# A unit's last product, issued behind the next unit's first two, in the gate/up loops of a two-layer trunk

## The chip, the cores and the metric

One core of a Trainium2 chip runs the whole program. The metric is device time in microseconds (us) for one execution. In the profile the engines are PE (TensorE matmul), PEld (TensorE's weight loads), DVE (VectorE), ACT (ScalarE), POOL (GpSimd) and SP, whose queue issues most of the loads.

## The reference, cut to what matters

A sequence of 512 tokens with 1024 channels passes two layers. Each layer is a token mixer and then a dense SwiGLU block; both sub-layers have an RMS norm before and after and a shift, a scale and a gate computed from a conditioning vector. The part that the change touches is the first half of the SwiGLU block, `silu(h @ w_gate) * (h @ w_up)`:

```python
D_MODEL, SEQ, D_FF = 1024, 512, 2816

def swiglu(h, w_gate, w_up, w_down):
    return (jax.nn.silu(h @ w_gate) * (h @ w_up)) @ w_down

    # in reference(), for each of the two layers i
    h = rms_norm(x, ffn_pre_g[i]) * (1.0 + scale) + shift
    y = swiglu(h, ffn_w_gate[i], ffn_w_up[i], ffn_w_down[i])
    x = x + gate * rms_norm(y, ffn_post_g[i])
```

All inputs are float32.

## The kernel before, in words

Every float32 operand is split into a high and a low part (`split`: ACT copies the high part to a `...h` tile, DVE subtracts to get the `...l` tile), and every product is three matmuls: high by high, high by low, low by high (`mm3`). Weights come from HBM in 512 KB blocks, on SP's queue, and are split on the way.

The gate and up matrices are cut into 22 blocks of 128 columns each. The first three blocks (`NH = 3`) go through `unit`, in the plain way. The other 19 go through `seven`, a Strassen-like scheme: for a pair (gate block, up block), seen as a 2 x 2 matrix of halves of the contraction by gate and up, and for the tokens in two halves of 256, seven products of half-size matrices take the place of eight. Each product is four slices of the contraction by three matmuls, so twelve matmuls of 128 x 128 weights by 256 tokens; a unit of seven products is 84 matmuls. The unit's weights are the raw halves (`x` and `b21`) and sums of them (`f13`, `f24`) that DVE makes and that are then split like the rest.

A unit uses three PSUM banks. `R1` takes A11·B11, then 2·T2 on top, then 3·T3 on top, then A22·T4 on top; `R2` takes A12·B21; `R3` takes 1·T1 and then 4·B22 on top. After most of these additions the running value is read: ACT copies `R1` and `R3` into the tile `e` (columns `s1`, `u1`, `s5`), and DVE makes four 256-column parts of `gu` from the bank and the copy. So the next product into a bank has to wait until its last reader is done. The last read before A22·T4 is DVE's `gu<-e,r`, the subtraction `s5 - R1`. A22·T4 stands in a function of its own, `rest`, which also takes the two silu's (ACT) and the product of gate and up (DVE, the tile `act`). In the kernel before, `run` calls `rest` at once after the other six products.

What sets the order: the program is written in one order, and a scheduler places each engine's instructions by their dependences, in an order fixed before the run. Where `pe["chain"]` is set, `pe_op` gives each matmul a dependence on the one written before it, so that TensorE keeps the written order; `dve.chain` and `act.chain` would do the same for their engines. None of them is set in the gate/up loops of the kernel before. Each engine then works through its own queue in order and waits on semaphores.

The loop also carries background work: after two of every three units, `bg0.step(1)` advances the computation of a modulation vector (the post-norm gate: a 512 KB load `rawada` into a slot, and a multiply-add `G<-rawada,sc,G` on DVE, eight of each in a loop, then two small splits and two pairs of 512-wide matmuls, `adaps`).

After the loop of layer 0 comes `out_proj` (the down projection, tiles `y`, weights `raw<-in_wdown`), in which two `rawada` loads are issued for each block of weights; after that of layer 1 comes `last` (tiles `X`, `M`).

In the traces all matmuls have line L90, all of DVE's and ACT's work has line L64, all DMA issues L107, and the three banks are all called `r`.

Of the kernel before, what the change touches and what calls it, by code (L numbers as in the profile page):

```python
# [25 lines left out]
def trunk(ctx: ExitStack, tc: tile.TileContext, A: dict, out: bass.AP):  # L26
# [16 lines left out]
    def nm(s):  # L43
        uid[0] += 1
        return f"{s}_{uid[0]}"

    def slot(dt, name, a=2, b=512):
        return s4.tile([P, a, b], dt, tag="s4", name=nm(name))

    def bank(name, tag="b"):  # L50
        return psum.tile([P, 512], F32, tag=tag, bufs=6 if tag == "b" else 2, name=nm(name))

    pe = {"prev": None, "chain": False}
# [47 lines left out]
    def mm3(o, lh, ll, rh, rl, start, stop):  # L101
        mm(o, lh, rh, start, False)
        mm(o, lh, rl, False, False)
        mm(o, ll, rh, False, stop)
# [101 lines left out]
    def wget(src, look=3):  # L206

        n = taken[0]
        taken[0] += 1
        while len(got) < min(n + 1 + look, len(stream)):  # L210
            wemit()
        assert stream[n][3] == src, (stream[n][3], src)
        return got[n]
# [200 lines left out]
    def hB(hT, k, lo, n):  # L414

        h, l = hT[lo // 256, k // 4]
        lo %= 256
        return h[:, k % 4, lo : lo + n], l[:, k % 4, lo : lo + n]
# [604 lines left out]
    def act_split(src):  # L1023
        t = slot(F32R, "as")
        split(t[:, 0, :], t[:, 1, :], src)
        return t[:, 0, :], t[:, 1, :]
# [5 lines left out]
    class Ffn:  # L1032
# [31 lines left out]
        def first(self):  # L1064
            return [lambda f=f: self.unit(f, 0, 256, 2 if f != 1 else 0) for f in range(NH)]

        def seven(self, f):

            W = wget(("blocks", (self.li, f - NH)), 1)
            R1, R2, R3 = [bank(n)[:, :256] for n in ("r1", "r2", "r3")]
            S = {n: (lambda k, t=self.S[n]: (t[0][:, k, :], t[1][:, k, :])) for n in "1234"}
            S["A11"] = lambda k: hB(self.hT, k, 0, 256)
            S["A12"] = lambda k: hB(self.hT, k + 4, 0, 256)
            S["A22"] = lambda k: hB(self.hT, k + 4, 256, 256)

            def product(o, a, b, start, stop):
                for k in range(4):  # L1080
                    h, l = S[a](k)
                    wh, wl = W[b](k)
                    mm3(o, wh, wl, h, l, start and k == 0, stop and k == 3)

            e = fpool.tile([P, 3, 256], F32, tag="e", name=nm("e"))
            gu = npool.tile([P, 2, T], F32, tag="n", name=nm("gu"))
            lo, hi = slice(0, 256), slice(256, T)
            s1, u1, s5 = [e[:, i, :] for i in range(3)]
            product(R1, "A11", "B11", True, False)
            act.activation(s1, R1, AF.Copy)  # L1090
            product(R2, "A12", "B21", True, True)
            dve.tensor_tensor(gu[:, 0, lo], R2, s1, ALU.add)
            product(R3, "1", "T1", True, False)
            act.activation(s5, R3, AF.Copy)
            product(R1, "2", "T2", False, False)
            act.activation(u1, R1, AF.Copy)
            product(R3, "4", "B22", False, True)
            dve.tensor_tensor(gu[:, 1, lo], R3, u1, ALU.subtract)
            product(R1, "3", "T3", False, False)
            dve.tensor_tensor(gu[:, 1, hi], s5, R1, ALU.subtract)  # L1100

            def rest():
                product(R1, "A22", "T4", False, True)
                act.activation(gu[:, 0, lo], gu[:, 0, lo], AF.Silu)
                last_act[0] = act.activation(gu[:, 0, hi], R1, AF.Silu)
                if f // 2 == len(self.act):
                    self.act.append(slot(F32, "act"))
                dve.tensor_tensor(
                    self.act[f // 2][:, f % 2, :], gu[:, 0, :], gu[:, 1, :], ALU.mult
                )  # L1110

            return rest

        def run(self, bg0, bg, bg2, steps, nhT, nxt, nS=None):
            for f in range(NH):
                self.unit(f, 256, 256)()
            for f in range(NH, KF):
                self.seven(f)()
                if f % 3:
                    bg0.step(1)  # L1120
            bg0.step(99)
            if self.li == 1:
                return self.last()
            out_proj(
                self.s, KF, lambda k: act_split(self.act[k // 2][:, k % 2, :]),
                lambda k: ("wdown", self.li, k), 4, bg, nhT, nxt, None, nS, steps, bg2,
            )


        def last(self):  # L1130
# [113 lines left out]
            for half in range(2):  # L1244
                X = [bank("X") for _ in range(NT)]
                M = [bank("M", "b" if i < 2 else "p") for i in range(4)]
                left = sum(k in "sx" for k, _ in LAST[half])
                tail = items[-NLAST:] if half else []
                while n < len(items) and items[n][0] == half and items[n] not in tail:
                    ahead(n)  # L1250
                    _, kind, j = items[n]
                    n += 1
                    if kind == "o":
                        plain(X, half, j, range(NT))
                    else:
                        seven(X, M, half, j, "mx" if kind == "s" else kind)
                        left -= kind != "m"
                        if left == 0:
                            K = joined(M)
                            left = -1  # L1260
                if half:
                    break
                junk = unread()
                for tt in range(NT):
                    dve.tensor_tensor(K[tt], X[tt][:], K[tt], ALU.add)
                    sq[0].append(small.tile([P, 1], F32, tag="sq0", name=nm("sq")))
                    act.activation(junk[:, halves[0]], K[tt], AF.Square, accum_out=sq[0][tt][:])
                    dve.tensor_tensor(K[tt], K[tt], ada["G", 3][:, halves[0]], ALU.mult)
                Y = K
# [271 lines left out]
```

## Time and profile before

| | |
|---|---|
| median of three runs | 1111.35 us |
| the profiled execution: its own time, and its span | 1111.05 us, 1109.3 us |
| PE busy | 1090.0 us, 98% of the span, 7318 matmuls |
| DVE, ACT busy | 902.3 us (81%), 603.1 us (54%) |
| gate/up loop of layer 0 | from 293.5 to 483.8 us |
| gate/up loop of layer 1 | from 797.5 to 988.2 us |
| granted TensorE clock, mean | 0.995 |

Matmuls are pipelined, so one of 256 columns is listed with 276 to 281 ns while the next one starts 113 to 118 ns after it; the pace is read from the starts of successive matmuls, not from their durations. A busy PE is for the same reason not a PE at its best pace. Idle time stands in front of the instruction that had to wait, with the name of what released it.

### The profile page before, as it was taken

How to read it: one execution, taken by the hardware profiler on the slowest of the kernel's cores; microseconds unless marked ns; L12 is line 12 of the kernel's file. 1: busy time of each engine (PE TensorE's matmuls, PEld its weight loads, DVE VectorE, ACT ScalarE, POOL GpSimd, SP SyncE). 2: the span in 40 equal slices, each digit the busy share in tenths (PEclk: the TensorE clock that was granted, in tenths of full speed). 3: DMA queues.
4: the chain of work that ended last, by engine and by line, in shares of the span. 5: the costliest groups of instructions: out<-in, count | busy, mean ns of one | idle time of the engine just before them, and what ended most of it. 6: DMA issues, size and time to landing. Idle time of an engine off the chain costs nothing.

```text
span 1109.3 us, 18286 instructions
## 1 busy us (share of the span) xinstructions
PE 1090.0 (98%) x7318; PEld 986.3 (89%) x7318; DVE 902.3 (81%) x1161; ACT 603.1 (54%) x977; POOL 39.7 (4%) x71
## 2 busy tenths in 40 slices
PE   7999999999999999999999999999999999999997
PEld 5788888789999999988878988989999999989896
DVE  7777889759998989797687774659988998889986
ACT  7746767646555555562244634437555555556552
POOL 0220111000000000010000000000000000000000
PEclk9999999999999999999999999999999999999999
DMA  9685445353344444378874582333244444223323
GB/s 362 234 240 161 147 144 163 135 190 134 97 132 153 151 138 131 96 239 266 281 254 174 181 287 87 110 130 134 79 153 129 138 134 153 76 77 109 102 95 152
DMA packets 51299, 176.09 MB, mean 159 GB/s; under 512 B 5644, under 2 KB 6156, under 8 KB 50319
## 3 DMA queue, kind: packets, MB, share of 16 engines
q1 hardware_dynamic: 45166, 153.95, 42.3%
q0 software_dynamic: 6048, 20.98, 6.0%
q8 instruction: 57, 0.93, 0.3%
q14 instruction: 28, 0.22, 0.1%
HBM read 164.43 MB, written 8.39 MB: 156 GB/s over the span
## 4 chain that ended last, share of the span: by engine, by line
PE 80%; DVE 7%; DMA 5%; issue 2%; ACT 2%; DVEq 0%; ACTq 0%
PE r L90 28%; PE y L90 11%; PE X L90 7%; PE pqk L90 7%; PE gu L90 6%; PE v L90 6%; PE u L90 4%; DMA rawada<-in_ada 3%; PE M L90 3%; PE z L90 2%; PE av L90 2%; DMA raw<-in_wdown 2%; PE tw L98 2%; DVE f L64 1%; DVE wl L64 1%
## 5 line engine op out<-in xcount | busy, mean ns | idle before, releaser
L64 ACT ACTIVATE wh<-raw 128x1024 fp32r<-128x1024 f32 (+1 forms) x112 | 117.1, 1053 | 132.4 <-DMA raw<-in_wdown 42.5
L64 DVE TENSOR_TENSOR wl<-raw,wh 128x1024 fp32r<-128x1024 f32 (+1 forms) x112 | 134.9, 1211 | 60.0 <-ACT wh L64 58.9
L90 PE MATMUL r<-Sh,wh 128*128 128x256 f32 x608 | 169.0, 278 | 0.4 <-ACT e L64 0.4
L90 PE MATMUL r<-Sh,wl 128*128 128x256 f32 x608 | 169.0, 278 | 0.0
L90 PE MATMUL r<-Sl,wh 128*128 128x256 f32 x608 | 168.9, 278 | 0.0
L90 PE MATMUL y<-wh,as 128*128 128x512 f32 x480 | 151.5, 393 | 0.0
L64 DVE TENSOR_TENSOR wl<-f,wh 128x1024 fp32r<-128x1024 f32 x76 | 92.8, 1221 | 35.5 <-ACT wh L64 35.5
L64 ACT ACTIVATE wh<-f 128x1024 fp32r<-128x1024 f32 x76 | 80.8, 1063 | 68.5 <-PE r L90 65.1
L90 PEld LDWEIGHTS r<-Sh,wl 128*128 128x128 f32 x608 | 114.8, 189 | 0.0
L90 PEld LDWEIGHTS r<-Sh,wh 128*128 128x128 f32 x608 | 114.3, 188 | 0.6 <-ACT e L64 0.6
L90 PEld LDWEIGHTS r<-Sl,wh 128*128 128x128 f32 x608 | 114.3, 188 | 0.0
L90 PEld LDWEIGHTS y<-wh,as 128*128 128x128 f32 x480 | 90.6, 189 | 18.9
L90 PE MATMUL y<-wl,as 128*128 128x512 f32 x240 | 94.2, 393 | 0.0
L90 PE MATMUL r<-hTh,wh 128*128 128x256 f32 x304 | 88.6, 291 | 1.2 <-DVE gu L64 0.6
L90 PE MATMUL r<-hTl,wh 128*128 128x256 f32 x304 | 84.4, 278 | 0.0
L90 PE MATMUL r<-hTh,wl 128*128 128x256 f32 x304 | 79.6, 278 | 0.0
L90 PE MATMUL X<-wh,as 128*128 128x512 f32 (+1 forms) x272 | 75.1, 353 | 0.0
L64 ACT ACTIVATE e<-r 128x256 f32<-128x256 f32 x114 | 43.3, 380 | 47.9 <-PE r L90 47.8
L90 PEld LDWEIGHTS r<-hTh,wh 128*128 128x128 f32 x304 | 57.2, 188 | 7.9 <-DVE gu L64 6.7
L64 ACT ACTIVATE wh<-rawx 128x1024 fp32r<-128x1024 f32 x38 | 40.4, 1063 | 35.8 <-PE r L90 30.0
L90 PE MATMUL r<-hTh,b 128*128 128x256 f32 x304 | 58.7, 278 | 0.0
L90 PEld LDWEIGHTS r<-hTl,wh 128*128 128x128 f32 x304 | 57.2, 188 | 0.1
(240 smaller groups left out, 2837.8 us busy)
## 6 DMA issues: line engine op xcount, KB each, us to landing
rawada<-in_ada SPq DMA_DIRECT2D x56, 512.0 KB, 4.6
raw<-in_wdown SPq DMA_DIRECT2D x44, 512.0 KB, 3.9
rawy<-in_wy SPq DMA_DIRECT2D x38, 512.0 KB, 3.6
rawx<-in_wx SPq DMA_DIRECT2D x38, 512.0 KB, 4.7
rawada<-in_ada POOLq DMA_DIRECT2D x24, 512.0 KB, 4.5
raw<-in_wqk SPq DMA_DIRECT2D x16, 512.0 KB, 3.9
ada<-in_ada0w SPq DMA_DIRECT2D x7, 1026.0 KB, 10.7
raw<-in_wgu SPq DMA_DIRECT2D x12, 512.0 KB, 3.6
```

Source lines behind the costliest of these rows:

```text
L64: b = f(*a, **k)
L90: b = nc.tensor.matmul(o, l, r, start=start, stop=stop, skip_group_check=True)
L98: last_tp[0] = nc.tensor.transpose(o, i, ident)
```

## The change

`seven` no longer issues its last product itself: `run` hands the `rest` of the unit before to it as `late`, and `seven` calls it behind the new unit's A11·B11 and A12·B21 and the reads that follow them. The last unit's `rest` is called after the loop. `pe["chain"]` is set for the whole loop, so that TensorE keeps the written order in it.

```diff
-        def seven(self, f):
+        def seven(self, f, late=None):
...
             act.activation(s1, R1, AF.Copy)
             product(R2, "A12", "B21", True, True)
             dve.tensor_tensor(gu[:, 0, lo], R2, s1, ALU.add)
+            if late is not None:
+                late()
             product(R3, "1", "T1", True, False)
...
             for f in range(NH):
                 self.unit(f, 256, 256)()
+            pe["chain"], late = True, None
             for f in range(NH, KF):
-                self.seven(f)()
+                late = self.seven(f, late)
                 if f % 3:
                     bg0.step(1)
+            late()
+            pe["chain"] = False
             bg0.step(99)
```

**TensorE at the first unit boundary of layer 0.** `r1_473` is the first bank of the first unit, `r1_490` that of the second, `r2_491` the second unit's second bank; `Sh`/`Sl` with `r1_473` is product 3·T3, `hTh_415`/`hTl_416` with `r1_473` is A22·T4, `hTh_358` is A11 and `hTh_361` is A12. Before:

```order
L90 MATMUL r1_473_2816<-Sh_455_2624,wl_433_2529 128x256
L90 MATMUL r1_490_2939<-hTh_358_2177,wh_439_2543 128x256
...
L90 MATMUL r1_490_2939<-hTl_359_2178,wh_439_2543 128x256
L90 MATMUL r1_473_2816<-hTh_415_2490,wh_435_2535 128x256
...
L90 MATMUL r1_473_2816<-hTh_415_2490,wl_436_2536 128x256
L90 MATMUL r1_490_2939<-hTh_358_2177,wl_440_2544 128x256
L90 MATMUL r2_491_2940<-hTh_361_2183,b210_441_2547 128x256
```

The scheduler had already put eleven of the twelve matmuls of the next A11·B11 between 3·T3 and A22·T4. In the changed kernel:

```order
L90 MATMUL r1_473_2816<-Sh_455_2624,wl_433_2529 128x256
L90 MATMUL r1_490_2924<-hTh_358_2177,wh_439_2543 128x256
...
L90 MATMUL r1_490_2924<-hTh_358_2177,wl_440_2544 128x256
L90 MATMUL r2_491_2925<-hTh_361_2183,b210_441_2547 128x256
...
L90 MATMUL r2_491_2925<-hTh_361_2183,b211_442_2548 128x256
L90 MATMUL r1_473_2816<-hTh_415_2490,wh_435_2535 128x256
...
L90 MATMUL r1_473_2816<-hTh_415_2490,wl_436_2536 128x256
L90 MATMUL r3_492_2926<-Sh_459_2628,wh_444_2553 128x256
```

Twenty-four matmuls now stand between 3·T3 and A22·T4, and the next thing behind it is 1·T1.

**ACT around the boundary between the second and the third unit.** `e<-r1` and `e<-r3` are the copies of a bank, `wh` and `b210` the high parts of the weights two units on, `gu` the two silu's. Before, from the second unit's copy of `R1`:

```order
L64 ACTIVATE e_493_2942<-r1_490_2939 128x256
L64 ACTIVATE wh_500_3047<-rawx_478_2914 128x1024
L64 ACTIVATE wh_505_3057<-f13_504_3055 128x1024
L64 ACTIVATE wh_508_3064<-f24_507_3061 128x1024
L64 ACTIVATE gu_494_2943<-r1_490_2939 128x256
L64 ACTIVATE e_513_3071<-r1_510_3068 128x256
L64 ACTIVATE b210_520_3177<-rawy_499_3044 128x512
L64 ACTIVATE e_513_3071<-r3_512_3070 128x256
L64 ACTIVATE gu_514_3072<-gu_514_3072 128x256
```

In the changed kernel:

```order
L64 ACTIVATE e_493_2927<-r1_490_2924 128x256
L64 ACTIVATE wh_499_3031<-rawx_478_2899 128x1024
L64 ACTIVATE wh_504_3041<-f13_503_3039 128x1024
L64 ACTIVATE e_512_3055<-r1_509_3052 128x256
L64 ACTIVATE b210_520_3162<-rawy_498_3028 128x512
L64 ACTIVATE gu_513_3056<-gu_513_3056 128x256
L64 ACTIVATE wh_507_3048<-f24_506_3045 128x1024
L64 ACTIVATE gu_494_2928<-r1_490_2924 128x256
L64 ACTIVATE e_512_3055<-r3_511_3054 128x256
```

The two steps that wait for A22·T4, `wh<-f24` (whose tile the product still reads) and the silu `gu<-r1`, have moved from in front of the next unit's copy of `R1` to directly in front of its copy of `R3`.

**SP's queue late in `out_proj` of layer 0.** `raw` are blocks of the down projection's weights, `rawada` blocks of the background work. Before:

```order
L107 DMA raw_913_5747<-in_wdown 128x1024
L107 DMA rawada_881_5616<-in_ada 128x1024
L107 DMA rawada_886_5652<-in_ada 128x1024
L107 DMA raw_922_5790<-in_wdown 128x1024
L107 DMA rawada_919_5782<-in_ada 128x1024
L107 DMA rawada_920_5784<-in_ada 128x1024
L107 DMA raw_927_5826<-in_wdown 128x1024
```

In the changed kernel:

```order
L107 DMA raw_913_5747<-in_wdown 128x1024
L107 DMA rawada_875_5577<-in_ada 128x1024
L107 DMA rawada_880_5613<-in_ada 128x1024
L107 DMA raw_922_5790<-in_wdown 128x1024
L107 DMA rawada_881_5616<-in_ada 128x1024
L107 DMA rawada_886_5652<-in_ada 128x1024
L107 DMA raw_927_5826<-in_wdown 128x1024
```

The pattern is the same, but each block of weights stands one pair of `rawada` loads earlier in the row.

## The prediction

> **What bounds the kernel now.** I read the page first: the busy times, then the chain of work that ended last.
>
> ```profile
> PE 1090.0 (98%) x7318; PEld 986.3 (89%) x7318; DVE 902.3 (81%) x1161; ACT 603.1 (54%) x977; POOL 39.7 (4%) x71
> PE 80%; DVE 7%; DMA 5%; issue 2%; ACT 2%; DVEq 0%; ACTq 0%
> ```
>
> TensorE is the bound, so the change can only win where it makes TensorE wait less or run at a closer pace. Next the view by windows, for the two gate/up loops.
>
> ```profile
> 293.50:481.00 187.50, 186.78 (x1589) 183.63 (x1588) 162.13 (x220) 105.22 (x177) 2.87 (x3) 1.00 0.43 133
> 797.50:986.00 188.50, 187.66 (x1589) 184.56 (x1588) 162.19 (x219) 103.79 (x172) 0.00 (x0) 1.00 0.38 124
> ```
>
> The columns are the stretch, its length, and the busy time (and count) of PE, PEld, DVE, ACT and POOL; then the granted clock, which is full. DVE is busy 162 of 187 us and ACT 105, so neither bounds the loop as a whole. The waits of the weight loads show the only wait that comes back unit after unit:
>
> ```profile
> PEld r L90 <- DVE gu L64: 6.7, 27, 0.4
> L90 PEld LDWEIGHTS r<-hTh,wh 128*128 128x128 f32 x304 | 57.2, 188 | 7.9 <-DVE gu L64 6.7
> ```
>
> That is 7.9 us of idle time, 0.2 us for each of 38 units. The timeline at one boundary shows where it stands, on TensorE and on DVE:
>
> ```profile
> 391.10 0.28 PE L90 MATMUL r<-Sh,wl 128*128 128x256 f32 x1
> 391.21 0.28 PE L90 MATMUL r<-hTh,wh 128*128 128x256 f32 x1
> ...
> 392.35 0.28 PE L90 MATMUL r<-hTl,wh 128*128 128x256 f32 x1
> 392.70 0.38 PE L90 MATMUL r<-hTh,wh 128*128 128x256 f32 x1
> 392.92 0.28 PE L90 MATMUL r<-hTl,wh 128*128 128x256 f32 x1
> 391.10 1.22 DVE L64 TENSOR_TENSOR wl<-rawx,wh 128x1024 fp32r<-128x1024 f32 x1
> 392.23 0.41 DVE L64 TENSOR_TENSOR gu<-e,r 128x256 f32<-128x256 f32 x1
> ```
>
> At 391.10 the last matmul of 3·T3 starts; eleven matmuls of the next unit follow; A22·T4 starts at 392.70, 0.06 us after DVE's subtraction has ended (392.23 + 0.41 = 392.64). DVE reaches that only behind a `wl` step. The stop costs twice: 0.35 us instead of about 0.113 in front of A22·T4, and 0.22 instead of 0.113 behind its first matmul, 0.34 us together here.
>
> There is a second thing in these loops, which shows only in the starts inside the units. Two stretches of four products (1·T1 to 3·T3, 48 matmuls, so 47 steps):
>
> ```profile
> 385.77 0.28 PE L90 MATMUL r<-Sh,wh 128*128 128x256 f32 x1
> 391.10 0.28 PE L90 MATMUL r<-Sh,wl 128*128 128x256 f32 x1
> 395.75 0.28 PE L90 MATMUL r<-Sh,wh 128*128 128x256 f32 x1
> 401.28 0.28 PE L90 MATMUL r<-Sh,wl 128*128 128x256 f32 x1
> ```
>
> The same work takes 5.33 us in one unit (113.4 ns a matmul, "close") and 5.53 in the next (117.7 ns, "wide"). The pace holds through a unit and changes only at a stop such as the one above: at 392.70 it goes from close to wide. A close matmul is listed with 276 ns, a wide one with 281:
>
> ```profile
> L90 PE MATMUL r<-Sh,wl 128*128 128x256 f32 x608 | 169.0, 278 | 0.0
> L90 PE MATMUL gu<-hTh,wh 128*128 128x256 f32 x192 | 54.3, 283 | 0.0
> 272.00:292.00 20.00, 20.00 (x172) 1.00 0.23 67
> ```
>
> The mean of 278 in the loops says that about (281 - 278)/5 = 0.6 of the matmuls run close. The plain `gu` units just before each loop, which have no such stop, are wide: (20.00 + 0.28)/172 = 117.9 ns in the last row, which is their window before the first loop.
>
> **The change part by part.** *The reorder.* A22·T4 moves from behind 12 to behind 25 steps after the last start of 3·T3. At the wide pace that is 391.10 + 25 x 0.1177 = 394.04 where DVE is done at 392.64: 1.34 us to spare after the 0.06. What could use that up is DVE, by the background products:
>
> ```profile
> L64 DVE SCALAR_TENSOR_TENSOR G<-rawada,sc,G x32: 1260/1280/1289, 68.4 to 924.6; 128x1024 f32<-128x1024 f32 x32
> ```
>
> A wide unit takes 84 x 0.1177 = 9.89 us. DVE works 162.13/187.5 x 9.89 = 8.5 us of it, 8 x 1.28/19 = 0.5 of that for the background. The changed order places two of these products in one unit, twice in a loop: 8.5 - 0.5 + 2.6 = 10.6 us in a unit of 9.89, 0.7 late, inside 1.34. So I expect no stop at any boundary.
>
> The loop without stops is then a matter of the pace. From the tile's rows by stretch, first and last start of each loop:
>
> ```profile
> L90 PE MATMUL r<-hTh,wh x152: 276/276/394, 293.5 to 483.6; 128*128 128x256 f32 x152
> L90 PE MATMUL r<-hTh,wl x152: 276/276/286, 293.7 to 483.8; 128*128 128x256 f32 x152
> L90 PE MATMUL r<-hTh,wh x152: 276/281/394, 797.5 to 988.0; 128*128 128x256 f32 x152
> L90 PE MATMUL r<-hTh,wl x152: 276/278/286, 797.7 to 988.2; 128*128 128x256 f32 x152
> 480.91 0.40 PE L90 MATMUL adaps<-acch,ones 128*128 128x512 f32 x1
> 481.14 0.40 PE L90 MATMUL adaps<-accl,ones 128*128 128x512 f32 x1
> ```
>
> The loops take 190.3 and 190.7 us for 19 x 84 = 1596 matmuls (1595 steps) and 8 and 6 others of 512 columns (four `adaps` and some `y` or `X`), at 481.14 - 480.91 = 0.23 us each: 1.8 and 1.4 us. With 60% close and 40% wide, the mean step is 115.1 ns and 1595 steps are 183.6 us, so the stops hold 190.3 - 1.8 - 183.6 = 4.9 us and 5.7 us, 10.6 us in all.
>
> But the close pace is itself a gift of the stops. Both loops come out of the `gu` units wide, and I see no unbroken stream of 256-column matmuls in this trace that turned close by itself. So I take the wide pace for all of the loop: 1595 x 117.7 = 187.7 us, and 189.5 and 189.1 with the others. The gain is 0.8 + 1.6 = 2.4 us, not 10.6. If the pace were close throughout it would be 1595 x 113.4 = 180.9 and a gain of 7.6 + 8.4 = 16.0.
>
> The page "TensorE: Matmul & The Clock Gate" of the Trainium skill, section "Back-to-back issue gap", gives one fixed gap for a warm stream, the columns over 2.4 GHz and 2.5 ns, an estimate of 109.2 ns for 256 columns; the trace has neither that figure nor a single one, and what one fixed gap would mean here is the first rival.
>
> *The chain on TensorE.* The scheduler had the same products in the same sequence but for A22·T4, and the `adaps` pairs stand at the same places (behind the 18th unit, and in front of the last A22·T4). At the end of the loop of layer 0 two `adaps` and five `y`, 7 x 0.23 = 1.6 us, cover the last A22·T4 as two and four did. Nothing for this.
>
> *ACT.* `wh<-f24` and the silu now stand in front of the copy `e<-r3`, which 4·B22 waits for. Here they are as they run now:
>
> ```profile
> 394.30 1.06 ACT L64 ACTIVATE wh<-f 128x1024 fp32r<-128x1024 f32 x1 [1.93 <-PE r L90]
> 395.26 0.37 ACT L64 ACTIVATE gu<-r 128x256 f32<-128x256 f32 x1
> 395.53 0.38 ACT L64 ACTIVATE e<-r 128x256 f32<-128x256 f32 x1
> ```
>
> From A22·T4's end they take 395.53 - 394.30 = 1.23 us to the start of the next step, and 1·T1, which `e<-r3` reads, ends twelve steps, 1.41 us, after A22·T4. So they fit under 1·T1 with 0.2 to spare; `e<-r3` then has 2·T2's 1.41 us for its 0.38, another 1.0. Nothing, as long as ACT is less than 1.2 us late.
>
> *Behind the loop of layer 0.* The loads in `out_proj` are in another order, and there is a wait there:
>
> ```profile
> 558.66 0.51 PE L90 MATMUL adaps<-acch,ones 128*128 128x512 f32 x1 [2.63 <-ACT acch L64]
> 558.60:563.00 4.40, 4.34 (x12) 0.61 0.71 247
> 550.94 1.06 ACT L64 ACTIVATE wh<-raw 128x1024 fp32r<-128x1024 f32 x1 [5.44 <-DMA raw<-in_wdown]
> 543.21 1.65 SPq L107 DMA_DIRECT2D rawada<-in_ada  x2
> 545.66 0.33 SPq L107 DMA_DIRECT2D raw<-in_wdown  x1
> ```
>
> TensorE waits 2.63 us for ACT, which is late because it waited 5.44 us for a block of weights whose load stood behind a pair of `rawada`; and the granted clock in the 4.4 us that follow is 0.61, another 0.39 x 4.4 = 1.7 us. In the new order that load stands one pair earlier, 545.66 - 543.21 = 2.45 us. This can take away nothing, the wait (2.6) or wait and clock (4.3), and if the pairs now delay something else, it can add as much as the wait again. I take 2.6, since the 2.45 us are nearest to that row; the range keeps -4.3 and +2.6.
>
> Sum: 1111.05 - 2.4 - 2.6 = 1106.05. The median of the runs shown is 0.3 above the profiled execution's time, so **1106.3 us**, 0.5% less. About 2%, 22 us, is what a measurement of this kernel can tell from no change.
>
> **The rivals.** *The stops go and the pace stays mixed* (or there is one fixed gap): the whole 10.6 us is won, 1111.05 - 10.6 - 2.6 = 1097.9. For it: a stop or two in a loop, by DVE where it has two background products, could turn the rest of the loop close. Against it: wide streams without stops stay wide. 0.22.
>
> *Close throughout*: 1111.05 - 16.0 - 2.6 = 1092.5. For it, only that the close pace can hold for a whole unit; against it, the loops enter wide. 0.07.
>
> *ACT becomes the wait*: `e<-r3` behind `wh<-f24` comes later than 4·B22 and TensorE stops there. It decides from 1.2 us of lateness on. DVE makes `f24`; a `wl` step (1.22) and a background product (1.28) in front of it together make ACT 2.5 late and TensorE 1.3, in the 16 units of both loops that have a background product: 20.8 us at most. With half of those the time is 1111.05 - 2.4 + 10.4 = 1119.1, slower than before. Against it: in the changed order `f24` is made some four products ahead of its use. 0.10.
>
> *The loads in `out_proj` collide worse* and the loop gives little: 1111.05 - 2.4 + 2.6 = 1111.3, no change. 0.06.
>
> **How the numbers follow.** The forecast has the remaining 0.55, with its own range from 1104 (wait and clock both gone) to 1109 (the wait stays). Leaving out the close case and ACT's, 0.17, the range goes from 1096 to 1112. No case but the worst of ACT's comes to 22 us: faster by over 2% 0.02 (every wait and the close pace together, under 1089), slower by over 2% 0.02, within 0.96.
>
> **What would show it.** Right: no idle time left in front of `r<-hTh,wh` for DVE's `gu`; all durations in the loops at 281 ns; loops of about 189 us each. A median of 276 would say that the pace is close, which is the likeliest way for me to be wrong. Stops in front of `r<-Sh,wh` for ACT's `e` would show ACT's rival. The `out_proj` term stands or falls with the 2.63 us in front of `adaps`.

## The result and the profile after

| | before | changed |
|---|---|---|
| median of the runs | 1111.26 us | 1137.03 us |
| the profiled execution, its span | 1111.05, 1109.3 us | 1137.21, 1135.4 us |
| gate/up loop of layer 0, first to last start | 190.3 us | 202.7 us |
| gate/up loop of layer 1 | 190.7 us | 202.1 us |
| between the two loops | 313.7 us | 315.0 us |

The changed kernel is slower: 1.023 times the time before, 95% interval 1.0215 to 1.0244. One of the six executions of the kernel before took 2190.41 us, for a reason that nothing here shows, and that ratio goes by the others. Of the 26.1 us by which the span grew, 12.3 and 11.4 lie in the two loops, 1.4 between them and 1.1 ahead of the first. So the change lost its time in the loops that it edits.

The chain of work that ended last was 80% TensorE before. On the page of the changed kernel it is this:

```profile
PE 56%; DVE 19%; DMA 13%; issue 6%; ACT 2%; DVEq 0%; ACTq 0%
PE y L90 10%; DMA rawx<-in_wx 8%; PE r L90 8%; PE X L90 7%; DVE wl L64 7%; PE pqk L90 7%; PE v L90 6%; PE u L90 4%; DMA rawada<-in_ada 4%; PE gu L90 3%; DVE f L64 3%; PE M L90 2%; DVE gu L64 2%; PE z L90 2%; PE av L90 2%
```

A load, `rawx<-in_wx`, is on it with 8% of the span, and the loops' matmuls (`PE r`) with 8%, where they had 28% before. `rawx` is one of the two raw blocks from which DVE makes a unit's sum `f13` (in the trace `f<-rawx,rawy`). The groups of the same page, with the idle time in front of each and what ended it:

```profile
L64 DVE TENSOR_TENSOR f<-rawx,rawy 128x1024 f32<-128x1024 f32 x38 | 46.3, 1223 | 57.4 <-DMA rawx<-in_wx 55.8
L90 PE MATMUL r<-hTh,wh 128*128 128x256 f32 x304 | 88.0, 290 | 18.4 <-DVE gu L64 18.1
L90 PE MATMUL r<-Sh,wh 128*128 128x256 f32 x608 | 170.6, 281 | 2.7 <-ACT e L64 2.5
```

DVE stood still for 57.4 us in front of its 38 `f13` additions, nearly all of it for the load. TensorE stood still for 18.4 us in front of A22·T4, for DVE's `gu`: the stop that the change was to remove, longer than before (1.2 us in the same row of the page before; in the row of its weight loads, by which the prediction measured the stop, 24.2 us where there were 7.9). The same `f13` group in the first loop alone, kernel before and then changed:

```profile
L64 DVE TENSOR_TENSOR f<-rawx,rawy 128x1024 f32<-128x1024 f32 x17 | 20.7, 1220 | 0.2 <-issue 0.2
```

```profile
L64 DVE TENSOR_TENSOR f<-rawx,rawy 128x1024 f32<-128x1024 f32 x17 | 20.8, 1224 | 28.7 <-DMA rawx<-in_wx 27.2 <-issue 1.6
```

The timelines say why. First the kernel before, DVE and SP's queue in one unit:

```profile
381.33 1.22 DVE L64 TENSOR_TENSOR wl<-rawx,wh 128x1024 fp32r<-128x1024 f32 x1
...
385.73 0.68 DVE L64 TENSOR_TENSOR act<-gu 128x512 f32<-128x512 f32 x1
386.33 1.22 DVE L64 TENSOR_TENSOR wl<-f,wh 128x1024 fp32r<-128x1024 f32 x1
...
388.40 0.69 DVE L64 TENSOR_TENSOR f<-f,rawx 128x512 f32<-128x512 f32 x1
389.02 1.23 DVE L64 TENSOR_TENSOR f<-rawx,rawy 128x1024 f32<-128x1024 f32 x1
390.16 0.68 DVE L64 TENSOR_TENSOR f<-f,rawy 128x512 f32<-128x512 f32 x1
382.57 0.33 SPq L107 DMA_DIRECT2D rawx<-in_wx  x1
```

`wl<-rawx` is the last reader of a raw block, and there are two buffers for `x`. When it ends (382.55), SP issues the load of the block two units on (382.57), and DVE adds that block at 389.02, 6.45 us after the issue. Now the changed kernel, the corresponding unit:

```profile
378.74 1.22 DVE L64 TENSOR_TENSOR wl<-rawx,wh 128x1024 fp32r<-128x1024 f32 x1
379.88 0.41 DVE L64 TENSOR_TENSOR gu<-e,r 128x256 f32<-128x256 f32 x1
380.21 1.22 DVE L64 TENSOR_TENSOR wl<-f,wh 128x1024 fp32r<-128x1024 f32 x1
381.34 0.42 DVE L64 TENSOR_TENSOR gu<-r,e 128x256 f32<-128x256 f32 x1
381.68 0.68 DVE L64 TENSOR_TENSOR b<-rawy,b 128x512 fp32r<-128x512 f32 x1
385.60 1.23 DVE L64 TENSOR_TENSOR f<-rawx,rawy 128x1024 f32<-128x1024 f32 x1 [3.24 <-DMA rawx<-in_wx]
386.74 1.22 DVE L64 TENSOR_TENSOR wl<-f,wh 128x1024 fp32r<-128x1024 f32 x1
387.88 0.68 DVE L64 TENSOR_TENSOR act<-gu 128x512 f32<-128x512 f32 x1
388.48 0.68 DVE L64 TENSOR_TENSOR f<-f,rawx 128x512 f32<-128x512 f32 x1
389.20 0.69 DVE L64 TENSOR_TENSOR f<-f,rawy 128x512 f32<-128x512 f32 x1
389.81 0.42 DVE L64 TENSOR_TENSOR gu<-r,e 128x256 f32<-128x256 f32 x1
390.14 1.22 DVE L64 TENSOR_TENSOR wl<-rawx,wh 128x1024 fp32r<-128x1024 f32 x1
391.28 0.41 DVE L64 TENSOR_TENSOR gu<-e,r 128x256 f32<-128x256 f32 x1
379.99 0.33 SPq L107 DMA_DIRECT2D rawx<-in_wx  x1
391.75 0.38 PE L90 MATMUL r<-hTh,wh 128*128 128x256 f32 x1 [1.59 <-DVE gu L64]
```

The load is issued at 379.99, again as soon as `wl<-rawx` is done, but DVE reaches the addition already at 382.36 (381.68 + 0.68), 2.4 us after the issue instead of 6.45. The median time of these loads from issue to landing is 4.7 us on the page before and 4.6 on the page of the changed kernel:

```profile
rawx<-in_wx SPq DMA_DIRECT2D x38, 512.0 KB, 4.7
rawx<-in_wx SPq DMA_DIRECT2D x38, 512.0 KB, 4.6
```

So 6.45 us cover the load and 2.4 do not. In DVE's queue the addition now stands ahead of `wl<-f24` (the `wl<-f` at 386.74), the silu product (`act<-gu`) and the two `f24` additions (`f<-f`); before it stood behind all of these but the second `f24` addition. DVE waits 3.24 us. Everything behind it in the queue moves back with it, down to `gu<-e,r` at 391.28, and A22·T4 starts at 391.75, 1.59 us late. `wl<-rawx`, at 390.14, is one of the steps moved back, and it is what releases the next load: each wait makes the next load late too.

The waits of the first loop, changed kernel:

```profile
ACT gu L64 <- DVE gu L64: 30.2, 18, 4.0
DVE f L64 <- DMA rawx<-in_wx: 27.2, 11, 3.7
PEld r L90 <- DVE gu L64: 11.9, 13, 2.1
PE r L90 <- DVE gu L64: 9.0, 11, 1.9
```

Eleven of the 17 additions wait, 2.5 us each on average. Behind one stop something more was lost: after the longest of this loop, 2.2 us from one start to the next at 414.06, the granted clock was 0.55 from 414.0 to 417.8 us and 16 matmuls came 209 to 214 ns apart, about 1.5 us more. The longest of the second loop, 3.4 us at 911.02, shows nothing of the kind. All this was read off one trace; the runs below test it.

### The profile page after: what moved, and what is told of

Read it like the earlier page. It is cut to its first block, busy times and chain, and to the rows that moved or that the text cites. A ratio compares the mean times of both kernels' runs of the same rounds, so it can differ in the third digit from the quotient of the medians.

```text
span 1135.4 us, 18239 instructions
## 1 busy us (share of the span) xinstructions
PE 1095.3 (96%) x7318; PEld 990.8 (87%) x7318; DVE 903.3 (80%) x1161; ACT 605.8 (53%) x977; POOL 39.7 (3%) x71
## 4 chain that ended last, share of the span: by engine, by line
PE 56%; DVE 19%; DMA 13%; issue 6%; ACT 2%; DVEq 0%; ACTq 0%
PE y L90 10%; DMA rawx<-in_wx 8%; PE r L90 8%; PE X L90 7%; DVE wl L64 7%; PE pqk L90 7%; PE v L90 6%; PE u L90 4%; DMA rawada<-in_ada 4%; PE gu L90 3%; DVE f L64 3%; PE M L90 2%; DVE gu L64 2%; PE z L90 2%; PE av L90 2%
## 5 line engine op out<-in xcount | busy, mean ns | idle before, releaser
L90 PE MATMUL r<-hTh,wh 128*128 128x256 f32 x304 | 88.0, 290 | 18.4 <-DVE gu L64 18.1
L64 DVE TENSOR_TENSOR f<-rawx,rawy 128x1024 f32<-128x1024 f32 x38 | 46.3, 1223 | 57.4 <-DMA rawx<-in_wx 55.8
L90 PE MATMUL r<-hTh,wl 128*128 128x256 f32 x304 | 85.3, 281 | 0.0
L90 PEld LDWEIGHTS r<-hTh,wh 128*128 128x128 f32 x304 | 57.8, 190 | 24.2 <-DVE gu L64 24.0
## 6 DMA issues: line engine op xcount, KB each, us to landing
ada<-in_ada0w SPq DMA_DIRECT2D x7, 1026.0 KB, 11.6
```

The source lines that it names most:

```text
L64: b = f(*a, **k)
L90: b = nc.tensor.matmul(o, l, r, start=start, stop=stop, skip_group_check=True)
```

## The experiments

**1. The addition put back.** On DVE alone, `f13`'s addition is held behind the second `f24` addition of the block before. TensorE keeps the changed order and its chain.

```diff
+    held = [None]
...
     def blocks(xr, yr):
...
         order(add, ready[0])
+        if held[0] is not None:
+            order(add, held[0])
...
-        dve.tensor_tensor(f24[:, 4:8, :], f24[:, 0:4, :], yr[:, 0:4, :], ALU.add)
+        held[0] = dve.tensor_tensor(f24[:, 4:8, :], f24[:, 0:4, :], yr[:, 0:4, :], ALU.add)
```

> The changed kernel with one order more: on VectorE the addition that makes a unit's f13 stands behind the second f24 addition of the unit before, so behind wl<-f24 and the silu product too; TensorE's order is the changed one. Theory (the load): in the changed kernel f<-rawx,rawy stands right behind the wl<-rawx that frees the buffer its load needs; the load takes about 4.8 us, VectorE waits for it (27.2 us idle in the first loop), and what is queued behind it makes the last product of a unit late. Then here the idle time of f<-rawx,rawy falls under 3 us in each loop, the stops in front of r<-hTh,wh under 2 us in both loops together (18.1 now), the loops take about 189 us each at the wide pace (202.7 and 202.2 now) and the kernel 1109 to 1113 us. Rival (ScalarE: silu and wh<-f24 in front of the copy e<-r3, or the moved product itself): the stops stay, loops of 198 us and more, 1125 to 1137 us. Second rival (the forecast's first rival: no stops, pace mixed): loops of 184 to 186 us, 1098 to 1103 us.

Measured: 1113.8 us, 1.0018 times before (1.0004 to 1.0032), 0.8 us above the expected range; the profiled execution, the fastest of its ten, took 1111.52. The `f13` group in the first loop, two TensorE groups of the page, and one group of matmuls by loop (shortest/median/longest duration, first to last start):

```profile
L64 DVE TENSOR_TENSOR f<-rawx,rawy 128x1024 f32<-128x1024 f32 x17 | 20.7, 1217 | 0.0
```

```profile
L90 PE MATMUL r<-Sh,wh 128*128 128x256 f32 x608 | 170.8, 281 | 0.0
L90 PE MATMUL r<-hTh,wh 128*128 128x256 f32 x304 | 85.6, 282 | 0.5 <-DVE gu L64 0.5
```

```profile
L90 PE MATMUL r<-hTh,wl x152: 276/281/286, 294.2 to 484.2; 128*128 128x256 f32 x152
L90 PE MATMUL r<-hTh,wl x152: 276/281/281, 799.0 to 988.7; 128*128 128x256 f32 x152
```

No wait for the load, no listed stop but one of 0.5 us (in front of the last product of the second loop), and no wait for ACT. These matmuls are the third of a unit, 0.24 us behind the first start, so the loops take 190.2 and 190.0 us (484.2 - 294.2 + 0.24, and the same for the second). All 24.6 us by which the changed kernel's loops are longer than these are gone, with TensorE's order untouched. The rivals (stops that stay, or a mixed pace) both fall.

**2. The load made earlier instead.** DVE's addition stays early; three buffers for each of the raw blocks let the load start about one unit earlier.

```diff
-    wraw = ctx.enter_context(tc.tile_pool(name="wraw", bufs=2))
+    wraw = ctx.enter_context(tc.tile_pool(name="wraw", bufs=3))
...
-    s4 = ctx.enter_context(tc.tile_pool(name="s4", bufs=28))
+    s4 = ctx.enter_context(tc.tile_pool(name="s4", bufs=26))
...
-    fwork["raw"] = ctx.enter_context(tc.tile_pool(name="wraw2", bufs=2))
+    fwork["raw"] = ctx.enter_context(tc.tile_pool(name="wraw2", bufs=3))
```

> The changed kernel with three buffers each for the raw weight blocks x and y where it has two, and 26 general slots where it has 28 to pay for them; the order of VectorE's steps in the loops keeps f<-rawx,rawy early, and TensorE's order is the same. Its load is now issued about one unit earlier. Theory (the load): no wait of f<-rawx,rawy (under 3 us a loop against 27.2), no stops in front of r<-hTh,wh, loops of about 189 us each; outside the loops the fewer slots may cost a few us, so 1107 to 1118 us. Rival (the order of VectorE's or ScalarE's steps as such, not the load): loops of 200 us and more as now, 1130 to 1140 us.

Measured: 1104.93 us, 0.9935 times before (0.9917 to 0.9954), 2.1 us under the expected range; experiment 5 shows where that comes from. The `f13` group in the first loop, and a group of matmuls by loop:

```profile
L64 DVE TENSOR_TENSOR f<-rawx,rawy 128x1024 f32<-128x1024 f32 x17 | 20.7, 1219 | 0.3
```

```profile
L90 PE MATMUL r<-hTh,wl x152: 276/281/281, 293.5 to 483.3; 128*128 128x256 f32 x152
L90 PE MATMUL r<-hTh,wl x152: 281/281/282, 793.1 to 982.3; 128*128 128x256 f32 x152
```

Loops of 190.0 and 189.4 us. The wait is gone (0.3 us), and so are the stops (0.0 us in front of `r<-hTh,wh`), though DVE's addition stands as early as in the changed kernel. So it was not DVE's or ACT's order as such, but a step that came to its load too soon. Two unlike cures with the same result in the loops settle the cause.

**3. The chain without the move.** Each unit's last product directly behind 3·T3.

```diff
-                late = self.seven(f, late)
+                self.seven(f)()
...
-            late()
```

> TensorE in written order, but each unit's last product directly behind 3 x T3, with nothing of the next unit in front. Theory: each unit's last product waits for VectorE's subtraction, which takes 0.41 us and stands behind a wl step of 1.22: a stop of 0.8 (VectorE free) to 1.7 us (VectorE still in the wl step) where the kernel before has 0.34 us; 36 boundaries, so 16 to 49 us more than before, 1127 to 1160 us, all of it in front of r<-hTh,wh. If the changed kernel's loss came from holding TensorE to the written order rather than from the load, this kernel would show at least that loss, 26 us, without any wait of f<-rawx,rawy for its load; by the theory the wait for the load may be there or not, since units of 11 us give it time.

Measured: 1154.54 us, 1.0381 times before (1.0361 to 1.0401). The group in front of which TensorE waits:

```profile
L90 PE MATMUL r<-hTh,wh 128*128 128x256 f32 x304 | 88.2, 290 | 44.3 <-DVE gu L64 44.3
```

44.3 us of stops, 1.2 us for each of 38 units, inside the 0.8 to 1.7 expected; the `f13` additions of its first loop wait for nothing. So a stop with no cover costs 1.2 us of idle time, the kernel before hides most of it behind one product, and the chain on TensorE is harmless only together with the move. By itself this run cannot tell the load from the chain: a loss of 26 us or more without any wait for the load is also what the chain as the cause was to show. Experiment 1 tells them apart, which has the chain and the move and loses nothing in the loops.

**4. One stop on purpose.** Experiment 1, with the last product of the first unit of each loop directly behind 3·T3. It asks what sets the pace.

```diff
                 late = self.seven(f, late)
+                if f == NH:
+                    late()
+                    late = None
```

> As the kernel with f13's addition held back, but the last product of the first unit of each loop stands directly behind 3 x T3, so that TensorE stops there once (about 1.5 us). It asks what sets the pace of the matmuls behind it. Theory (the pace changes only at a stop and then holds): if the stop turns the pace close, some 16 units run at 113.4 instead of 117.7 ns up to the 512-column adaps, 16 x 84 x 4.3 ns = 5.8 us less a loop, less the stop: 1101 to 1105 us where the kernel without the stop has 1109 to 1113; if the stop leaves it wide, 1111 to 1116 us. Rival (the pace drifts or hangs on something else): changes of pace inside units, without a stop in front of them.

Measured: 1109.35 us, 0.9974 times before (0.9961 to 0.9987), which lies between the two ranges that were expected for a close and for a wide pace. The profiled execution took 1106.06 us where that of experiment 1 took 1111.52; each is the fastest of its ten, and what the slower ones did no profile shows. A group of matmuls by loop, and TensorE's timeline at the stop of the first loop, the last matmul of 3·T3 and the first of A22·T4:

```profile
L90 PE MATMUL r<-hTh,wl x152: 276/276/286, 294.8 to 481.4; 128*128 128x256 f32 x152
L90 PE MATMUL r<-hTh,wl x152: 276/276/282, 797.0 to 983.3; 128*128 128x256 f32 x152
```

```profile
302.94 0.28 PE L90 MATMUL r<-Sh,wl 128*128 128x256 f32 x1
304.38 0.39 PE L90 MATMUL r<-hTh,wh 128*128 128x256 f32 x1 [1.16 <-DVE gu L64]
```

The median duration turns from 281 to 276 ns by one stop a loop. Read from the starts, every matmul of that loop ahead of 304.38 comes 117.8 ns after the one before it (on average), and in each of the next six units all 84 come after 113.3 ns: 9.52 us a unit instead of 9.89, with no stop among them. The loops take 186.8 and 186.5 us. The gain of 3.4 and 3.5 us is less than the 4.3 expected: short stops come back from the eighth unit on, when at the close pace DVE has only 9.52 us for a unit (that this brings them back is argued, not tested). Behind the 512-column `adaps` the pace is wide again. The rival, a pace that drifts without a stop, finds almost nothing for it: six matmuls from 387.96 on come 116 to 122 ns apart without a listed stop, and then the pace is 113.3 again.

**5. The buffers alone.** The kernel before, with the buffers of experiment 2 and nothing else.

> The kernel before with the three raw buffers each and the 26 general slots of the buffers' run, nothing else. It separates what the buffers do by themselves from what the changed order does once its load is in time. Theory: the loops keep their stops at each unit boundary (190 to 191 us each); the stretch between the loops falls from 313.7 to about 310 us, because the wait in front of adaps goes, as it does in the buffers' run (309.6 us); 1107 to 1109 us. If so, the changed order is worth 0.3 (first loop) and 1.4 us (second loop) there: 190.0 and 189.4 us against 190.3 and 190.7, so 1.7 us of the 7 between that run and the kernel before. Rival (the buffers' gain needs the changed order): 1111 us or more.

Measured: 1106.22 us, 0.9937 times before (0.9923 to 0.9951), 0.8 us under the expected range. A group of matmuls by loop, and two of TensorE's groups in a stretch of `out_proj`, first of the changed kernel (20 us of it) and then of this one (40 us):

```profile
L90 PE MATMUL r<-hTh,wl x152: 276/281/283, 293.1 to 484.9; 128*128 128x256 f32 x152
L90 PE MATMUL r<-hTh,wl x152: 276/276/286, 794.1 to 983.3; 128*128 128x256 f32 x152
```

```profile
L90 PE MATMUL y<-wh,as 128*128 128x512 f32 x36 | 12.4, 414 | 1.6 <-DVE as L64 1.6
L90 PE MATMUL adaps<-accl,ones 128*128 128x512 f32 x3 | 1.6, 527 | 2.6 <-DVE accl L64 2.6
```

```profile
L90 PE MATMUL y<-wh,as 128*128 128x512 f32 x108 | 34.7, 392 | 0.0
L90 PE MATMUL adaps<-accl,ones 128*128 128x512 f32 x6 | 2.4, 404 | 0.0
```

Between the loops 309.0 us, without a wait in `out_proj`: the buffers by themselves bring that stretch to where experiment 2 has it (309.6), from 313.7 before. The loops take 192.0 and 189.4 us, together 2.0 more than experiment 2's (expected was 1.7), and as whole kernels the two cannot be told apart (0.9937 and 0.9935 of the time before). So with its load in time the changed order is worth next to nothing by itself: it trades stops at a pace that is often close for no stops at the wide one.

**6. Buffers and one short stop.** Experiment 2, and in each loop the first unit's last product behind only six matmuls of the next unit, so that TensorE stops once.

```diff
-            def product(o, a, b, start, stop):
+            def product(o, a, b, start, stop, between=None):
                 for k in range(4):
+                    if k == 2 and between is not None:
+                        between()
...
-            product(R1, "A11", "B11", True, False)
+            if f == NH + 1:
+                product(R1, "A11", "B11", True, False, late)
+                late = None
+            else:
+                product(R1, "A11", "B11", True, False)
```

> The changed kernel with three raw buffers each and 26 slots, and one stop in each loop: the last product of the first unit stands behind six matmuls of the next unit, everywhere else behind two products. Theory (a stop sets the pace and it holds): a stop of about 0.7 us, then 113.3 ns a matmul up to the adaps of 512 columns, some 15.9 units of 84 matmuls x 4.4 ns = 5.9 us; loops of 184.8 and 184.2 us instead of 190.0 and 189.4, 1104.9 - 10.4 = 1094.5 us. Rival (a stop this short leaves the pace wide): 1105 to 1107 us.

Measured: 1098.86 us, 0.9861 times before (0.9841 to 0.9882), where 1094.5 us were expected; two executions took 1093.5 us, three 1099. The profiled one took 1093.58:

```profile
L90 PE MATMUL r<-hTh,wl x152: 276/276/281, 293.6 to 477.7; 128*128 128x256 f32 x152
L90 PE MATMUL r<-hTh,wl x152: 276/276/282, 787.3 to 970.8; 128*128 128x256 f32 x152
```

Loops of 184.3 and 183.7 us, 5.7 less than without the stop (5.2 expected): the matmuls run close from the stop to the first pair of `adaps`, 1332 of them in the first loop, with no further stop. The stop itself came out shorter than the 0.7 us expected: in each loop the first matmul of A22·T4 starts 0.27 us after the one before it, and the next 0.22 us later.

**7 and 8. A longer stop, and a second look.** The two groups of experiment 6 called for an explanation. Experiment 7 is experiment 2 with the last product placed as in experiment 4, which makes a step of 0.98 us from start to start (1.44 in experiment 4); experiment 8 is experiment 6 once more.

> As the run with the buffers and a stop, but the first unit's last product stands directly behind 3 x T3, so the one stop of each loop is about 1.5 us instead of 0.7. That run's five executions fell into two groups, 1093.5 us (two, the profiled one among them) and 1099 us (three), 5.5 us apart, which is about what one loop gains by the close pace (5.9). Theory (a short stop turns the pace close in some executions only, loop by loop, and a longer one more surely): all executions within 2 us of 1095. Rival (whether the pace turns is chance, whatever the stop's length): groups near 1095 and 1100.5 us again, perhaps 1106 too. Third (the spread has to do with something outside the loops): groups again, with both loops close in every profile.

> The run with the buffers and a stop once more, the same kernel, to see another execution's profile. If the time is near 1099 us: by the theory one loop shows 117.8 ns a matmul behind its stop (190 us long) and the other 113.3 (184 us); by the third view of the run beside it both loops are 184 us long and the 5.5 us lie elsewhere. If it is near 1093.5 us, both loops are again 184 us long and nothing is told apart.

Measured: experiment 7 took 1094.4 to 1094.6 us three times and 1106.1 once (median 1094.48, 0.9864 of before, 0.9806 to 0.9921); experiment 8 took 1092.87, in the profiled execution, and 1094.24 (0.9821, 0.9794 to 0.9848; with two executions it is open whether that is 2%). Both profiles have both loops close (185.1 and 184.4 us, 184.4 and 183.7 us), so neither shows an execution of a higher group. The groups lie 5.5 and 11.6 us apart, about one loop's gain and both loops' gain; that in those executions a stop left one loop or both wide would explain it, but no profile caught it, so it stays open. Against the theory that a longer stop is surer stands the one execution at 1106.1. Experiment 6's kernel is faster than the kernel before in all of its seven executions, by 14 to 21 us of the 1113 us that the kernel before took beside it.

## Why the prediction was wrong, by its own steps

**What bounds the kernel**: right as far as it went. TensorE was the bound and the stops at the unit boundaries were there. Experiment 3 shows their full price without cover.

**The reorder**: this step failed. It asked what could use up the 1.34 us of margin, and answered "DVE, by the background products", counting DVE's work: 8.5 us in a unit of 9.89. The work did fit. What it left out is that DVE's queue also holds a step that waits for a load, that the load is released by another step of the same queue, and that the change moved the one closer to the other: from 6.45 to 2.4 us behind the issue. The step looked at the order on TensorE and ACT and never at where `f13` had gone on DVE. The margin itself was about right: at the first two boundaries of the changed kernel's first loop, ahead of the first late load, A22·T4 starts 1.54 and 1.34 us after the subtraction's end, and in experiment 1 mostly 1.22. The waits, up to 3.7 us and in most units, were too long for it.

**The loop without stops goes wide**: right. In experiment 1 the units take 9.89 us each, to the digit of the forecast, and the loops 190.2 and 190.0 us where 189.5 and 189.1 were predicted. Part of the rest is the last boundary of the second loop, where A22·T4 still waits:

```profile
987.33 0.39 PE L90 MATMUL r<-hTh,wh 128*128 128x256 f32 x1 [0.48 <-DVE gu L64]
```

So the wide pace, not the stops, decided that the move could gain little: without the stops the two loops are 0.8 us shorter than before, not 10.6. The rival of one fixed gap (1097.9 us) falls in experiment 1, whose stream without stops holds 117.8 ns. The Trainium skill's page "TensorE: Matmul & The Clock Gate", section "Back-to-back issue gap", gives the columns over 2.4 GHz and 2.5 ns, an estimate of 109.2 ns here, as the gap of an isolated warm matmul, and says that in a stream where each matmul has its weight load both set the spacing; the prediction took the figure for that of a stream. No run here has 109.2 ns, and the measurements decide. The close rival (1092.5 us) was set aside because a loop enters wide, which holds until something stops it: experiment 6 is that case, with its one stop bought.

**The chain**: nothing, as said; experiment 1 has it and loses nothing in the loops. **ACT**: the sign named for its rival did appear, stops in front of `r<-Sh,wh` for `e` (2.7 us), but as a consequence. ACT waited 30.2 us in the first loop for DVE's `gu`, and with the load in time the stops for `e` are 0.0.

**The term behind the loop**: wrong in sign, inside its bounds. It took 2.6 us off; the stretch between the loops grew by 1.4. The wait in front of `adaps` stayed, now for DVE's `accl`, and a new one came ahead of it:

```profile
566.61 1.28 DVE L64 SCALAR_TENSOR_TENSOR G<-rawada,sc,G 128x1024 f32<-128x1024 f32 x1 [1.60 <-DMA rawada<-in_ada]
569.68 0.30 PEld L90 LDWEIGHTS y<-wh,as 128*128 128x128 f32 x2 [2.08 <-DVE as L64]
```

Here too DVE stands for a load, of `rawada`, and TensorE waits for the `as` queued behind it. With the buffers TensorE waits 0.2 us in that stretch in experiment 2, which has the changed order, and not at all in experiment 5.

What else the sum missed shows in experiment 1, the change without the load's wait: its profiled execution took 1111.5 us, which is the sum's 1106.05, plus 1.6 for the loops' remainder, 3.5 for the stretch between the loops (314.6 us instead of 313.7 less 2.6) and 0.4 for the start of the first loop (293.9 instead of 293.5). So by that execution the forecast would have been 5.5 us too low even without the wait.

## What to carry to other kernels

When a change makes a scheduler reorder an engine's queue, look in it for the steps that wait for a load, and measure the distance from the step that frees the load's buffer to the step that uses it; a margin counted in busy time says nothing about a queue that waits for a load it releases itself. Where such a distance falls under the load's time, hold the step back or add a buffer, and test both, since two different cures with one result settle a cause better than one. And price a stream without stops by the pace that it will run at, not by the stops alone.

## What the hardware showed that was not expected

The same 256-column matmuls have two steady paces at a granted clock of 1.00, 113.3 and 117.8 ns, and keep either for well over a thousand of them (1416 wide in experiment 1, 1332 close in experiment 6). In the loops the pace changed behind a stop or a 512-column matmul, with two exceptions: the six matmuls of experiment 4, and one boundary of the changed kernel (466.75), where the stream turned from wide to close behind a step of 121 ns, with no stop listed. A stop put on purpose, of 0.27 us (experiments 6 and 8), 0.98 (7) or 1.44 us (4) from one start to the next, turned the stream behind it from 117.8 to 113.3 ns in every loop of the four profiles that have one, and with the shortest a loop came out 5.7 us shorter, the stop included. Stops by themselves do not always do it: among the changed kernel's stops some turned a close stream wide, and the higher times of experiments 6 and 7 are not explained. Why there are two paces, and what in a stop chooses one, no run here shows.
